# A gated delta rule at the head of a two-block network: inverses by blocks of 16 instead of 32, with the projections rearranged around them

## Chip, cores, metric

One core of a Trainium2 chip runs the whole program. The metric is the device time of one execution in microseconds, taken as the median of several runs.

## The reference, cut to what matters

The network maps 256 tokens of width 1024 through two blocks. The first layer is a gated delta net with 8 heads of width 128: four projections (q, k, v, z) of 1024 columns each, a causal depthwise convolution of 4 taps with Silu on q, k and v, the delta rule, and an output norm gated by Silu(z). All of it is fp32.

```python
proj = hn @ w_in
qkv = silu(causal_depthwise_conv(proj[..., :3072], conv_w))
z = proj[..., 3072:4096]
...
gc = cumsum(g, axis=-1)
decay = exp(where(tri_incl, gc[..., :, None] - gc[..., None, :], -inf))
a_low = where(tri_strict, einsum('bhncd,bhnsd->bhncs', k_beta, k) * decay, 0.0)
a_mat = a_low + eye(c)
sol = triangular_solve(a_mat, concat([v * beta, k_beta * exp(gc)]), lower=True, unit_diagonal=True)
...
o = rmsnorm(o, out_norm_g) * silu(z)
return o.reshape(b, t, DN_DIM) @ w_out
```

Behind it come an MLP, a block attention, a second MLP, and a second block of four mixers (among them a gated 31-tap convolution whose gate is a sigmoid, a forgetting attention and a differential attention), a cross attention and a gated MLP.

## The kernel before

Every linear layer goes through `lin` (L241) and `group`. A weight tile of 128 x 1024 (two k-slices of 512 columns) is loaded by the SP queue into `wr`, and `weight` splits it into a high part `wh` (a copy on ACT, L77) and a low part `wl` (a subtraction on DVE, L57); three matmuls per block (L53) then make up one fp32 product. The ring of weights has 4 `wr` and 5 `wh`/`wl` buffers. A group of 512 columns is four such tiles, 96 matmuls, and accumulates in two `acc` banks of PSUM. In the delta net there are just two `acc` banks, so a group can't start before the group ahead of it has been taken out of both. The other six banks (`ps`) serve everything else. The order of each engine's queue is made by a scheduler from the program order (its priorities), `later(n)` (a lower priority by n) and `after(...)` (an instruction of the same engine that has to be issued before). Each engine then works its queue in order.

The stages of `delta_net` (L447) are, in program order: `gates`; `decays` for the four pairs of (group of four heads, chunk of 128 tokens), which makes the matrix M of decays; the two k groups of projections; `unit_keys` and `gram`, which make A, 16 matrices of 128 x 128 (8 heads, 2 chunks); `inverses`; `level_64` and `level_128`; the q and v groups; `intra` (M times the products of k and q); `tokens`; `outputs`; the two z groups under `later(300)` and `later(600)`; and the output projection.

`inverses` (L567) takes the 32 x 32 blocks on the diagonal of A through HBM (`ga`, DMAs of the POOL queue) into `at`, each block on two partitions (one for its even columns, one for its odd ones), and inverts all 64 of them at once on DVE. It makes 31 steps of two dependent instructions each (`tmp`, `zt`). The result goes back through HBM (`gz`) into Z. `level_64` and `level_128` then fill the blocks below: each call transposes Z (`turned`, L600: four transposes on PE, a copy `X` on ACT), multiplies A by Z, copies `Y` on ACT, multiplies by X, and writes the negated product into Z on ACT. There are eight such calls.

`conv_pair` (L505) is what takes a q, k or v bank out: a copy into `pad` (2 buffers, their three leading columns set to zero on POOL each time), a scaled copy of the bank into `cy`, six multiply-adds on DVE (L60), and a Silu on ACT. `on_z` (L718) takes a z bank out by a clamp on DVE, Exp, Ln and Exp on ACT, and a multiply on DVE that reads the bank once more. ACT has one table of functions at a time. `table` (L271) loads the one that holds both Ln and Exp; Silu and the Sigmoid of the second block's gate (`gate` in `long_conv`, L1150) need others.

Of the kernel before, what the change touches and what calls it, by code (L numbers as in the profile page):

```python
# [16 lines left out]
P = 128  # L17
T = 256
D = 1024
KD = D // P  # L20
# [4 lines left out]
class Net:  # L25
# [421 lines left out]
    def delta_net(self):  # L447
        nc, tc, a = self.nc, self.tc, self.a
        W = a["dn_w_in"][0]
        H, d = 8, 128  # L450
        banks = self.ctx.enter_context(ExitStack())
        banks.enter_context(self.banks(2))
        with ExitStack() as ctx:
            dp = ctx.enter_context(tc.tile_pool(name="dn", bufs=1, reuse_waits="tile"))
# [46 lines left out]
            Z = core.tile([P, 16, P], F32, name="Z")  # L501
            nc.gpsimd.memset(Z, 0.0)
            four = lambda t, g, c: t[:, (g * 2 + c) * 4:(g * 2 + c) * 4 + 4, :]

            def conv_pair(col, o, dst, behind):  # L505
                t = col // P
                pad = dp.tile([P, 2, T + 3], F32, tag="pad", name="pad", bufs=2)
                nc.gpsimd.memset(pad[:, :, 0:3], 0.0)
                self.copy(pad[:, :, 3:], o)
                y = dp.tile([P, 2, T], F32, tag="cy", name="cy", bufs=2)  # L510
                w = lambda j, i: cw[:, j * 24 + t + i:j * 24 + t + i + 1]
                for i in range(2):
                    self.act(y[:, i, :], o[:, i, :], AF.Copy, scale=w(3, i))
                for j in range(3):
                    for i in range(2):
                        self.stt(y[:, i, :], pad[:, i, j:j + T], w(j, i), y[:, i, :], OP.mult, OP.add)
                with self.after(*behind):
                    self.last_silu = self.act(dst, y, AF.Silu)

            def project(dst, tag, base, g, behind):  # L520
                dst[g] = dp.tile([P, 4, T], F32, tag=tag, name=tag, bufs=2)
                base += g * 512
                self.lin(W, KD, [(base, 512)], rd, lambda col, o: conv_pair(
                    col, o, dst[g][:, (col - base) // P:(col - base) // P + 2, :], behind))

# [8 lines left out]
            def decays(g, c):  # L534

                h4 = slice(g * 4, g * 4 + 4)
# [30 lines left out]
            def inverses(sv):  # L567


                ga = hbm.tile([4, 16, 32, 32], F32, name="ga")  # L570
                gz = hbm.tile([4, 16, 32, 32], F32, name="gz")
                for b in range(4):
                    r = slice(32 * b, 32 * b + 32)
                    nc.gpsimd.dma_start(ga[b].rearrange("m i j -> i m j"), A[r, :, r])
                at = sv.tile([P, 32, 32], F32, name="at")
                for s in range(2):
                    nc.gpsimd.dma_start(at[s * 64:s * 64 + 64], ga.rearrange("b m i j -> (b m) i j"))
                zt = sv.tile([P, 16, 32], F32, name="zt")
                zi = sv.tile([P, 16, 32], I32, name="zi")
                nc.gpsimd.iota(zi, pattern=[[-2, 16], [1, 32]], base=0, channel_multiplier=0)  # L580
                zf = sv.tile([P, 16, 32], F32, name="zf")
                nc.gpsimd.tensor_copy(zf, zi)
                for s in range(2):
                    r = slice(s * 64, s * 64 + 64)
                    self.ts(zt[r], zf[r], float(s), None, OP.is_equal, eng=nc.gpsimd)
                tmp = sv.tile([P, 160], F32, name="tmp")
                for j in range(31):
                    n, m = j // 2 + 1, 31 - j
                    u = tmp[:, 0:n * m].rearrange("p (c i) -> p c i", i=m)
                    self.tt(u, zt[:, 0:n, j:j + 1].to_broadcast([P, n, m]),  # L590
                            at[:, j + 1:32, j][:, None, :].to_broadcast([P, n, m]), OP.mult)
                    self.tt(zt[:, 0:n, j + 1:32], zt[:, 0:n, j + 1:32], u, OP.subtract)
                to = gz.rearrange("b m (c s) i -> s (b m) c i", s=2)
                for s in range(2):
                    nc.gpsimd.dma_start(to[s], zt[s * 64:s * 64 + 64])
                for b in range(4):
                    r = slice(32 * b, 32 * b + 32)
                    nc.gpsimd.dma_start(Z[r, :, r], gz[b].rearrange("m c i -> c m i"))

            def turned(zz):  # L600
                X = big("X", 2)
                p = self.ps()
                for i in range(4):
                    nc.tensor.transpose(p[:, i * P:(i + 1) * P], zz[:, i, :], self.ident)  # L604
                self.copy(X, v4(p))
                return X

            def level_64(A, zz):
# [31 lines left out]
            def intra(g, c):  # L640

                cs = slice(c * P, (c + 1) * P)
                m = M[g, c]
                self.tt(m, m, b4(self.tri[:, 0:P]), OP.mult)
                p = self.ps()
                mm4(p, lambda i: (k[g][:, i, cs], q[g][:, i, cs]))
                self.tt(m, v4(p), m, OP.mult)
                if c == 1:
                    self.tt(qd[g], q[g][:, :, cs], qd[g], OP.mult)

            def tokens(g):

                h4 = slice(g * 4, g * 4 + 4)
                for c in range(2):
# [17 lines left out]
            def outputs(g):  # L672
# [22 lines left out]
                for j in range(2):  # L695
# [12 lines left out]
                    zj = z[:, g * 4 + 2 * j:g * 4 + 2 * j + 2, :]  # L708
                    self.tt(zj, o, zj, OP.mult)
# [3 lines left out]
                    self.rsqrt_wide(r, self.pairs(p), d, oeps)  # L713
                    self.tt(zj, zj, r, OP.mult)
# [3 lines left out]
            def on_z(col, o):  # L718
                h = col // P - 24
                zj = z[:, h:h + 2, :]  # L720
                e = dp.tile([P, 2, T], F32, tag="ze", name="ze", bufs=1)
# [22 lines left out]
            late = ctx.enter_context(tc.tile_pool(name="late", bufs=1, reuse_waits="tile"))  # L744
            for level in (level_64, level_128):
                for g, c in both:
                    level(four(A, g, c), four(Z, g, c))
            project(q, "q", 0, 0, behind)
            project(q, "q", 0, 1, behind)
            project(vt, "vt", 2048, 0, behind)  # L750
            project(vt, "vt", 2048, 1, behind)
            pin = self.table(self.last_silu)
            for g, c in both:
                intra(g, c)
            tokens(0)
            step = lambda it: next(it, None)
            out = [outputs(g) for g in range(2)]
            step(out[0])
            with self.later(300):
                self.lin(W, KD, [(3072, 512)], rd, on_z)  # L760
            step(out[0])
            step(out[0])
            xo[0] = (late.tile([P, 4, T], F32R, name="xoh"), late.tile([P, 4, T], F32R, name="xol"))
            with self.later(600):
                self.lin(W, KD, [(3584, 512)], rd, on_z)
            xo[1] = self.new_xg(0)
# [297 lines left out]
    def mixers(self, xg, rows, bp):  # L1064
# [539 lines left out]
```

## Time and profile before

| what | value |
|---|---|
| median of 3 runs | 1304.67 us (1304.06 to 1305.09) |
| the profiled execution | 1303.15 us |
| its span, first to last instruction | 1301.4 us |
| PE busy | 1256.0 us (97%) |
| DVE busy | 866.7 us (67%) |
| ACT busy | 739.0 us (57%) |
| POOL busy | 21.1 us (2%) |
| mean granted TensorE clock | 0.979 |
| moved by DMA | 207.31 MB, mean 159 GB/s |

Busy times overlap, so they don't add up to the span. A matmul's end is modelled, so a busy PE isn't yet a PE at its peak: the granted clock says how fast it ran (1.00 is 2.4 GHz, 0.50 is 1.2 GHz). The delta net fills the first 233 us of the span.

### The profile page before, as it was taken

The page shows a single profiled execution, that of the slowest core. Times are in us where ns is not written, and L with a number is a line of the kernel's source. Part 1 is how long each engine was busy: PE and PEld are TensorE (multiplying, and loading weights), DVE is VectorE, ACT ScalarE, POOL GpSimd, SP SyncE. Part 2 cuts the span into 40 slices and gives each one's busy share as a digit, 9 for nine tenths or more (in the row PEclk, how much of TensorE's full clock was granted, in tenths as well). Part 3 has the DMA queues.
Part 4 walks back from the last instruction along what each step waited for, and adds up shares of the span by engine and source line. Part 5 has one row for each costly group of instructions (what it writes and reads, how often), then busy time and mean ns, then how long its engine had stood idle before and what let it go on. Part 6 is the DMA issues. An engine that isn't in the chain of part 4 may idle for free.

```text
span 1301.4 us, 23746 instructions
## 1 busy us (share of the span) xinstructions
PE 1256.0 (97%) x9656; PEld 1196.5 (92%) x9656; DVE 866.7 (67%) x1388; ACT 739.0 (57%) x1132; POOL 21.1 (2%) x68
## 2 busy tenths in 40 slices
PE   7997789999999999999999999999999999999998
PEld 6997678999999999999999988799999998999997
DVE  6799236644546665744445998998556684977775
ACT  5874536654545445854545755665447565756554
POOL 2010100000000000000000000000000000000000
PEclk8998679999999999999999999999999999999999
DMA  6454303666664744656562553446664642665652
GB/s 202 143 171 146 82 1 115 227 189 189 184 181 143 224 140 142 208 171 185 179 190 69 166 176 99 145 134 192 183 190 147 203 169 65 204 201 173 184 177 83
DMA packets 99632, 207.31 MB, mean 159 GB/s; under 512 B 9694, under 2 KB 12292, under 8 KB 99524
## 3 DMA queue, kind: packets, MB, share of 16 engines
q1 hardware_dynamic: 98114, 202.85, 50.6%
q0 software_dynamic: 928, 2.88, 0.9%
q8 instruction: 75, 1.23, 0.4%
q14 instruction: 33, 0.27, 0.1%
q10 hardware_dynamic: 482, 0.08, 0.0%
HBM read 204.21 MB, written 1.57 MB: 158 GB/s over the span
## 4 chain that ended last, share of the span: by engine, by line
PE 83%; DVE 9%; ACT 3%; DMA 3%; issue 2%; POOL 0%; DVEq 0%; SPq 0%; ACTq 0%; POOLq 0%
PE acc L53 51%; PE ps L53 30%; DVE wl L57 2%; DVE yc L60 1%; ACT wh L77 1%; DMA wr<-in_mlp_w_up_dram 1%; PE ps L604 1%; DVE xl L60 1%; PE ps L894 1%; DVE sq L57 0%; DMA wr<-in_dn_w_in_dram 0%; DMA wr<-in_w_xkv_dram 0%; DMA xt<-in_x_dram 0%; DMA gz<-zt 0%; DVE tmp L57 0%
## 5 line engine op out<-in xcount | busy, mean ns | idle before, releaser
L57 DVE TENSOR_TENSOR wl<-wr,wh 128x1024 fp32r<-128x1024 f32 (+1 forms) x384 | 466.3, 1219 | 297.4 <-ACT wh L77 296.7
L77 ACT ACTIVATE wh<-wr 128x1024 fp32r<-128x1024 f32 (+1 forms) x384 | 402.3, 1053 | 387.4 <-PE acc L53 235.9
L53 PE MATMUL acc<-xh,wh 128*128 128x256 f32 (+1 forms) x1064 | 305.8, 288 | 7.8 <-DVE z L60 5.1
L53 PE MATMUL acc<-xh,wl 128*128 128x256 f32 (+1 forms) x1064 | 304.1, 287 | 3.5 <-DVE wl L57 3.5
L53 PE MATMUL acc<-xl,wh 128*128 128x256 f32 (+1 forms) x1064 | 303.8, 286 | 0.8 <-DVE xl L57 0.8
L53 PE MATMUL ps<-xh,wh 128*128 128x256 f32 (+1 forms) x872 | 248.1, 285 | 4.7 <-DVE x L57 2.5
L53 PE MATMUL ps<-xh,wl 128*128 128x256 f32 (+1 forms) x872 | 247.4, 284 | 1.8 <-DVE wl L57 1.8
L53 PE MATMUL ps<-xl,wh 128*128 128x256 f32 (+1 forms) x872 | 247.4, 284 | 0.5 <-DVE xl L57 0.3
L53 PEld LDWEIGHTS acc<-xh,wh 128*128 128x128 f32 (+1 forms) x1064 | 204.4, 192 | 11.5 <-issue 6.5
L53 PEld LDWEIGHTS acc<-xh,wl 128*128 128x128 f32 (+1 forms) x1064 | 204.3, 192 | 5.1 <-DVE wl L57 3.7
L53 PEld LDWEIGHTS acc<-xl,wh 128*128 128x128 f32 (+1 forms) x1064 | 204.7, 192 | 2.1 <-DVE xl L57 1.2
L53 PEld LDWEIGHTS ps<-xh,wh 128*128 128x128 f32 (+1 forms) x872 | 166.4, 191 | 6.0 <-DVE x L57 2.7
L53 PEld LDWEIGHTS ps<-xh,wl 128*128 128x128 f32 (+1 forms) x872 | 166.4, 191 | 2.4 <-DVE wl L57 2.0
L53 PEld LDWEIGHTS ps<-xl,wh 128*128 128x128 f32 (+1 forms) x872 | 166.5, 191 | 1.5 <-DVE xl L57 1.1
L53 PE MATMUL acc<-hh,wh 128*128 128x256 f32 x512 | 144.6, 283 | 0.0
L53 PE MATMUL acc<-hh,wl 128*128 128x256 f32 x512 | 144.3, 282 | 0.0
L53 PE MATMUL acc<-hl,wh 128*128 128x256 f32 x512 | 144.2, 282 | 0.0
L53 PEld LDWEIGHTS acc<-hh,wl 128*128 128x128 f32 x512 | 97.3, 190 | 0.0
L53 PEld LDWEIGHTS acc<-hh,wh 128*128 128x128 f32 x512 | 97.2, 190 | 0.0
L53 PEld LDWEIGHTS acc<-hl,wh 128*128 128x128 f32 x512 | 97.1, 190 | 0.0
L60 DVE SCALAR_TENSOR_TENSOR yc<-cpad,vec_b,yc 128x256 f32<-128x256 f32 x120 | 51.3, 480 | 0.1
L60 DVE SCALAR_TENSOR_TENSOR fy<-pad,vec_b,fy 128x256 f32<-128x256 f32 x88 | 36.7, 479 | 0.0
(430 smaller groups left out, 1744.7 us busy)
## 6 DMA issues: line engine op xcount, KB each, us to landing
wr<-in_mlp_w_up_dram SPq DMA_DIRECT2D x64, 512.0 KB
wr<-in_mlp_w_down_dram SPq DMA_DIRECT2D x64, 512.0 KB
wr<-in_w_in_dram SPq DMA_DIRECT2D x44, 512.0 KB
wr<-in_w_up_dram SPq DMA_DIRECT2D x44, 512.0 KB
wr<-in_dn_w_in_dram SPq DMA_DIRECT2D x32, 512.0 KB
wr<-in_w_gate_dram SPq DMA_DIRECT2D x32, 512.0 KB
wr<-in_mb_w_in_dram SPq DMA_DIRECT2D x24, 512.0 KB
wr<-in_w_down_dram SPq DMA_DIRECT2D x22, 512.0 KB
```

What stands on the lines that cost most here:

```text
L53: self.last_mm = self.nc.tensor.matmul(out, lhsT=lhsT, rhs=rhs, start=start, stop=stop, skip_group_check=True)
L57: return (eng or self.nc.vector).tensor_tensor(out=out, in0=a, in1=b, op=op)
L60: return self.nc.vector.scalar_tensor_tensor(out, a, s, b, op0=op0, op1=op1, **kw)
L77: a = self.nc.scalar.activation(hi, src, AF.Copy)
L604: nc.tensor.transpose(p[:, i * P:(i + 1) * P], zz[:, i, :], self.ident)
L894: self.nc.tensor.transpose(pt[:, i * P:(i + 1) * P], p[:, i * P:(i + 1) * P], self.ident)
```

## The change

The blocks that DVE inverts become 16 x 16: 15 steps instead of 31, 128 blocks, one per partition, and `at` shrinks to 16 columns. A third level, `level_32`, joins the blocks of 16 on PE. It takes its factors from a new tile L, which four more DMAs of the POOL queue fill from A, and `gz` is first set to zero by a DMA. The convolution works in place in its destination, out of six `pad` tiles that are zeroed once; its multiply-adds for the second q group and both v groups are held on DVE until the last step of the inverse (`hold`). z becomes one Silu out of the bank, and its norm weight moves into `outputs`. `intra` moves: group 0 ahead of the levels, group 1 behind `level_32`; its mask multiply goes to POOL, behind the last DMA of the inverse. `decays` and `tokens` put work of DVE on ACT, four instructions of 128 x 128 for one of 128 x 512. The first z group is `later(200)`, the second waits on PE for the first transpose of `level_32`. One table load follows z's Silus, and one follows the second block's sigmoids.

```diff
+            L = core.tile([P, 16, 32], F32, name="L")
+            pads = [dp.tile([P, 2, T + 3], F32, name=f"pad{i}") for i in range(6)]
...
-            def conv_pair(col, o, dst, behind):
+            def conv_pair(col, o, dst, behind, hold):
                 t = col // P
-                pad = dp.tile([P, 2, T + 3], F32, tag="pad", name="pad", bufs=2)
-                nc.gpsimd.memset(pad[:, :, 0:3], 0.0)
+                pad = pads[t // 2 % len(pads)]
                 self.copy(pad[:, :, 3:], o)
-                y = dp.tile([P, 2, T], F32, tag="cy", name="cy", bufs=2)
+                y = dst
...
-                    self.act(y[:, i, :], o[:, i, :], AF.Copy, scale=w(3, i))
+                    self.act(y[:, i, :], pad[:, i, 3:], AF.Copy, scale=w(3, i))
+                with self.after(*hold):
...
                         self.stt(y[:, i, :], pad[:, i, j:j + T], w(j, i), y[:, i, :], OP.mult, OP.add)
...
-                self.tt(m, v4(p), tok(gc[:, c, h4]), OP.subtract)
+                for i in range(4):
+                    self.act(m[:, i, :], p[:, i * P:(i + 1) * P], AF.Abs, scale=-1.0, bias=gc[:, c, g * 4 + i:g * 4 + i + 1])
...
-                self.act(m, m, AF.Abs)
...
+                nc.gpsimd.dma_start(gz.rearrange("b m i j -> (b m) (i j)"), Z[0:64].rearrange("p m i -> p (m i)")[:, 0:1024])
...
+                for b in range(4):
+                    r = slice(32 * b + 16, 32 * b + 32)
+                    nc.gpsimd.dma_start(L[r, :, 0:16], A[r, :, 32 * b:32 * b + 16])
...
-                for j in range(31):
-                    n, m = j // 2 + 1, 31 - j
+                for j in range(15):
+                    n, m = j + 1, 15 - j
...
+            def level_32(L, zz):
+                X = turned(zz)
+                p = self.ps()
+                rows = [slice(r, r + 32) for r in range(0, P, 32)]
+                for i in range(4):
+                    for r in rows:
+                        self.mm(p[r, i * 32:(i + 1) * 32], L[r, i, :], zz[r, i, r], True, True)
+                v = lambda p: p[:, 0:128].rearrange("p (h e) -> p h e", e=32)
+                Y = big("Y", 2)
+                self.copy(Y[:, :, 0:32], v(p))
+                p = self.ps()
+                for i in range(4):
+                    for r in rows:
+                        self.mm(p[r, i * 32:(i + 1) * 32], X[r, i, r], Y[r, i, 0:32], True, True)
+                for r in range(0, P, 32):
+                    self.act(zz[r:r + 16, :, r + 16:r + 32], v(p)[r:r + 16, :, 16:32], AF.Copy, scale=-1.0)
...
-                self.tt(m, m, b4(self.tri[:, 0:P]), OP.mult)
...
+                with self.after(self.back):
+                    self.tt(m, m, b4(self.tri[:, 0:P]), OP.mult, nc.gpsimd)
...
-                    self.tt(kx[c], v4(p), tok((beg if c else kdec)[:, h4]), OP.mult)
+                    for i in range(4):
+                        h = g * 4 + i
+                        self.act(kx[c][:, i, :], p[:, i * P:(i + 1) * P], AF.Copy, scale=(beg if c else kdec)[:, h:h + 1])
...
-                self.ts(e, o, -80.0, None, OP.max)
-                with tc.issue_after(pin.ins):
-                    self.act(e, e, AF.Exp, scale=-1.0)
-                self.act(e, e, AF.Ln, bias=1.0)
-                self.act(e, e, AF.Exp, scale=-1.0)
-                self.stt(zj, o, self.vec["onorm"], e, OP.mult, OP.mult)
+                with self.after(*behind):
+                    silus.append(self.act(z[:, h:h + 2, :], o, AF.Silu))
...
+            project(q, "q", 0, 0, behind)
+            hold = self.solved,
+            project(q, "q", 0, 1, behind, hold)
+            project(vt, "vt", 2048, 0, behind, hold)
+            project(vt, "vt", 2048, 1, behind, hold)
+            for c in range(2):
+                intra(0, c)
+            turns, silus = [], []
+            for level, src in ((level_32, L), (level_64, A), (level_128, A)):
                 for g, c in both:
-                    level(four(A, g, c), four(Z, g, c))
+                    level(four(src, g, c), four(Z, g, c))
+                    turns.append(self.last_turn)
+                if src is L:
+                    for c in range(2):
+                        intra(1, c)
+            with self.later(200):
+                self.lin(W, KD, [(3072, 512)], rd, on_z)
+            with self.after(turns[0]):
+                self.lin(W, KD, [(3584, 512)], rd, on_z)
+            with self.after(*silus):
+                pin = self.table(silus[-1])
             tokens(0)
...
-                    self.act(sg[:, m + i, :], sg[:, m + i, :], AF.Sigmoid, bias=V["b_glu"][:, 4 + m + i:5 + m + i])
+                    last = self.act(sg[:, m + i, :], sg[:, m + i, :], AF.Sigmoid, bias=V["b_glu"][:, 4 + m + i:5 + m + i])
+                if m == 2:
+                    self.table(last)
```

## Rows read from the trace of the kernel before

**Rows 1.** The page, busy time of the engine that fills the span

```profile
PE 1256.0 (97%) x9656; PEld 1196.5 (92%) x9656; DVE 866.7 (67%) x1388; ACT 739.0 (57%) x1132; POOL 21.1 (2%) x68
```

**Rows 2.** Busy time by stretch: stretch, length, busy (instructions) per engine, clock, DMA

```profile
91.05:102.83 11.78, 11.77 (x96) 11.56 (x96) 11.78 (x35) 7.80 (x12) 0.21 (x2) 1.00 0.16 49
102.83:143.82 40.99, 26.92 (x192) 26.20 (x193) 33.18 (x72) 20.02 (x27) 4.26 (x6) 0.89 0.61 176
143.82:172.20 28.38, 24.50 (x225) 19.39 (x225) 0.75 (x1) 12.54 (x33) 0.00 (x0) 0.50 0.02 7
172.20:178.20 6.00, 6.00 (x39) 6.00 (x39) 2.50 (x4) 0.38 (x1) 0.00 (x0) 0.70 0.00 0
178.20:229.20 51.00, 46.38 (x358) 42.39 (x357) 30.48 (x46) 28.23 (x43) 1.23 (x3) 1.00 0.27 83
```

**Rows 3.** The chain that ended last, 91 to 103 us: start, us, what

```profile
91.05 11.78 PE acc L53 x96
```

**Rows 4.** The same chain, 131 to 147 us

```profile
131.22 0.79 POOL gz L595
132.01 4.99 DMA gz<-zt
...
137.59 1.96 POOL Z L598 x3
139.55 4.14 DMA Z<-gz
143.82 1.10 PE ps L604 x4
...
145.83 0.87 PE ps L53 x16
```

**Rows 5.** DVE by groups of instructions, 87.3 to 131 us: count, busy, mean ns

```profile
L57 DVE TENSOR_TENSOR wl<-wr,wh 128x1024 fp32r<-128x1024 f32 x11 | 13.7, 1246 | 0.3 <-ACT wh L77 0.2
L60 DVE SCALAR_TENSOR_TENSOR cy<-pad,vec_a,cy 128x256 f32<-128x256 f32 x24 | 12.2, 510 | 0.3 <-ACT cy L70 0.3
L57 DVE TENSOR_TENSOR tmp<-zt,at 128x126 f32<-128x126 f32 (+22 forms) x31 | 10.5, 339 | 0.3
L57 DVE TENSOR_TENSOR zt<-zt,tmp 128x126 f32<-128x126 f32 (+22 forms) x31 | 8.4, 270 | 0.3
```

**Rows 6.** DVE in order of time: start, us, instruction

```profile
78.89 4.84 DVE L60 SCALAR_TENSOR_TENSOR cy<-pad,vec_a,cy 128x256 f32<-128x256 f32 x12 [0.36 <-ACT cy L70]
...
87.38 0.21 DVE L57 TENSOR_TENSOR tmp<-zt,at 128x31 f32<-128x31 f32 x1
...
129.03 0.26 DVE L57 TENSOR_TENSOR tmp<-zt,at 128x56 f32<-128x56 f32 x1
...
129.57 0.21 DVE L57 TENSOR_TENSOR tmp<-zt,at 128x45 f32<-128x45 f32 x1
```

**Rows 7.** DVE and POOL in order of time, 203 to 206 us

```profile
203.94 1.22 DVE L57 TENSOR_TENSOR wl<-wr,wh 128x1024 fp32r<-128x1024 f32 x1
...
204.83 0.69 POOL L145 CAST df<-di 128x384 f32<-128x384 int32 x1
```

**Rows 8.** ACT by groups of instructions, 0 to 300 us

```profile
L70 ACT ACTIVATE m<-m 128x512 f32<-128x512 f32 x8 | 4.7, 623 | 0.9 <-DVE m L57 0.9
L73 ACT ACTIVATE vec_b<-ps 128x128 f32<-128x128 f32 (+1 forms) x4 | 0.9, 261 | 0.0
```

**Rows 9.** POOL by groups of instructions, 0 to 215 us

```profile
L65 POOL TENSOR_SCALAR zt<-zf 64x512 f32<-64x512 f32 x2 | 3.0, 1496 | 0.2
...
L582 POOL CAST zf<-zi 128x512 f32<-128x512 int32 x1 | 0.6, 607 | 0.1
```

**Rows 10.** ACT in order of time, in the second block's differential attention

```profile
840.79 1.28 ACT L70 ACT_TABLE_LOAD   x1
...
842.79 1.28 ACT L70 ACT_TABLE_LOAD   x1
```

**Rows 11.** PE in order of time, the same stretch

```profile
846.45 0.30 PE L894 MATMUL ps<-ident,s 128*128 128x128 f32 x1 [2.65 <-DVE s L60]
```

More of the change, by code (lines that the diff above doesn't have):

```diff
@@ L502, in delta_net, with project @@
             nc.gpsimd.memset(Z, 0.0)
+            L = core.tile([P, 16, 32], F32, name="L")
+            nc.gpsimd.memset(L, 0.0)
+            pads = [dp.tile([P, 2, T + 3], F32, name=f"pad{i}") for i in range(6)]
+            for pad in pads:
+                nc.gpsimd.memset(pad[:, :, 0:3], 0.0)
             four = lambda t, g, c: t[:, (g * 2 + c) * 4:(g * 2 + c) * 4 + 4, :]
-            def conv_pair(col, o, dst, behind):
+            def conv_pair(col, o, dst, behind, hold):
                 t = col // P
-                pad = dp.tile([P, 2, T + 3], F32, tag="pad", name="pad", bufs=2)
-                nc.gpsimd.memset(pad[:, :, 0:3], 0.0)
+                pad = pads[t // 2 % len(pads)]
                 self.copy(pad[:, :, 3:], o)
-                y = dp.tile([P, 2, T], F32, tag="cy", name="cy", bufs=2)
+                y = dst
                 w = lambda j, i: cw[:, j * 24 + t + i:j * 24 + t + i + 1]
                 for i in range(2):
-                    self.act(y[:, i, :], o[:, i, :], AF.Copy, scale=w(3, i))
-                for j in range(3):
-                    for i in range(2):
+                    self.act(y[:, i, :], pad[:, i, 3:], AF.Copy, scale=w(3, i))
+                with self.after(*hold):
+                    for j, i in [(j, i) for j in range(3) for i in range(2)]:
                         self.stt(y[:, i, :], pad[:, i, j:j + T], w(j, i), y[:, i, :], OP.mult, OP.add)
                 with self.after(*behind):
-                    self.last_silu = self.act(dst, y, AF.Silu)
-            def project(dst, tag, base, g, behind):
+                    self.last_silu = self.act(y, y, AF.Silu)
+            def project(dst, tag, base, g, behind, hold=()):
                 dst[g] = dp.tile([P, 4, T], F32, tag=tag, name=tag, bufs=2)
@@ L523, in project @@
                 self.lin(W, KD, [(base, 512)], rd, lambda col, o: conv_pair(
-                    col, o, dst[g][:, (col - base) // P:(col - base) // P + 2, :], behind))
+                    col, o, dst[g][:, (col - base) // P:(col - base) // P + 2, :], behind, hold))
             def big(tag, bufs, pool=None):
@@ L582, in inverses @@
-                nc.gpsimd.tensor_copy(zf, zi)
[L583 to L586, printed above, removed]
-                for j in range(31):
-                    n, m = j // 2 + 1, 31 - j
+                at = sv.tile([P, 16, 32], F32, name="at")
+                flat = ga.rearrange("b m i j -> (b m) (i j)")
+                for h in range(2):
+                    r = slice(h * 64, h * 64 + 64)
+                    nc.gpsimd.dma_start(at[r].rearrange("p i j -> p (i j)")[:, 0:496], flat[:, h * 528:h * 528 + 496])
@@ L594, in inverses @@
-                for s in range(2):
-                    nc.gpsimd.dma_start(to[s], zt[s * 64:s * 64 + 64])
+                            at[:, j + 1:16, j][:, None, :].to_broadcast([P, n, m]), OP.mult)
+                    self.solved = self.tt(zt[:, 0:n, j + 1:16], zt[:, 0:n, j + 1:16], u, OP.subtract)
+                for h in range(2):
+                    q = slice(16 * h, 16 * h + 16)
+                    nc.gpsimd.dma_start(gz[:, :, q, q].rearrange("b m c i -> (b m) c i"), zt[h * 64:h * 64 + 64])
@@ L596, in inverses @@
                 for b in range(4):
                     r = slice(32 * b, 32 * b + 32)
-                    nc.gpsimd.dma_start(Z[r, :, r], gz[b].rearrange("m c i -> c m i"))
+                    self.back = nc.gpsimd.dma_start(Z[r, :, r], gz[b].rearrange("m c i -> c m i"))
             def turned(zz):
@@ L712, in outputs @@
                     r = dp.tile([P, 2, T], F32, tag="kr", name="kr", bufs=1)
-                    self.rsqrt_wide(r, self.pairs(p), d, oeps)
+                    with tc.issue_after(pin.ins):
+                        self.rsqrt_wide(r, self.pairs(p), d, oeps)
                     self.tt(zj, zj, r, OP.mult)
@@ L757, in delta_net @@
             out = [outputs(g) for g in range(2)]
[L758 to L762, printed above, removed]
+            for _ in range(3):
+                step(out[0])
             xo[0] = (late.tile([P, 4, T], F32R, name="xoh"), late.tile([P, 4, T], F32R, name="xol"))
-            with self.later(600):
-                self.lin(W, KD, [(3584, 512)], rd, on_z)
             xo[1] = self.new_xg(0)
```

31 lines of the change are left out of this document (8 added, 23 removed).

## The prediction, made before the changed kernel ran

> **What bounds it now.** I read the page first: PE is busy for 97% of the span [rows 1], so time can be won only where PE stands still or runs at its lower clock. The stretches of the delta net, read by their clock, show where that is [rows 2]. From 91.05 to 102.83 us PE is full at the full clock: the last v group is 96 matmuls in 11.78 us [rows 3]. Between 102.83 and 143.82 it is busy for only 26.92 of 40.99 us, at a clock of 0.89. From 143.82 to 172.20, in the eight calls of the two levels, the clock is 0.50 throughout, and to 178.20, in `intra`, 0.70. After that it is full again. Third, the chain of waits says what PE waited for: the last step of the inverse, then `gz` out (issue at 131.22, landed by 137.0), `Z` back (landed by 143.7), and only then the first transpose [rows 4]. So the inverse sets when the levels start. Fourth, DVE from 87.3 to 131 us: the inverse itself is 10.5 + 8.4 = 18.9 us of work [rows 5], drawn out to some 43 us, because 24 multiply-adds of the convolution (12.2 us) and 11 splits (13.7 us) stand between its steps. By 143.8 us the z groups, PE's only other work (the 192 matmuls of that stretch, [rows 2]), are used up, so the levels run alone, and at half clock.
>
> The sum is made on the profiled execution, 1303.15 us for a span of 1301.4. It lies 1.52 us under the median of 1304.67, and I add that at the end. About 0.2%, 2.6 us, is what a measurement of this kernel can tell from no change.
>
> **The inverse and its way back.** Thirty-one steps become 15, with at most 8 x 8 = 64 elements. A step of 56 elements takes 129.57 - 129.03 = 0.54 us from start to start [rows 6]. I use it for all 15: 8.1 us. The held multiply-adds can't come between, the splits can: three of 1.22 us [rows 7], as the ring fills, make 11.8 us. Group 0's products for `intra` may add 1 us. The start stays at 87.4 us [rows 6]. Two things move it, and I let them cancel: `at` no longer queues on POOL behind a zeroing of `pad` that waits for DVE, and `decays` puts four instructions of 128 x 128 on ACT (some 4 x 0.26 us) in place of one Abs of 0.62 us [rows 8], four times, 1.7 us more on the way to A. So the inverse ends at 99 us, and the issue of `gz` follows there rather than at 131.22. The way back costs what it does now, 143.82 - 131.22 = 12.6 us [rows 4]: as many pieces, half as long. The bound is 11 to 14 us. Z is there at 112 us. The four DMAs for L and the zeroing of `gz` lie beside the 15 steps on POOL's queue. I cost them at nothing. Without that cover they would cost four issues of about 0.65 us each, as the three in [rows 4].
>
> **The stall that the hold makes.** `pads[t // 2 % 6]` gives q's second group pads 2 and 3 (t // 2 = 2, 3) and v's first group pads 2 and 3 again (t // 2 = 8, 9). So v's first group can't be copied out of its banks until the held multiply-adds of q have run, and with two `acc` banks the last v group can't start. That group started at 91.05 us [rows 3]. Now it waits for 99 us, plus half of the 4.84 us that twelve multiply-adds take [rows 6], plus a copy of some 0.6 us [rows 8]: 102.0 us for the first bank, 104.4 for the second. As the first bank gives PE 12 matmuls, 1.5 us, the group ends at 104.4 + 11.78 - 1.5 = 114.7 us. What is behind v's copy on ACT's queue waits too, weight splits above all, but PE has no use for them then. Only group 0 of `intra` fits into the hole.
>
> **What PE has to do from there.** Two z groups: 2 x 11.78 = 23.6 us [rows 3]. The old levels: 24.50 us busy at a clock of 0.50 [rows 2], so 12.2 at 1.00. `level_32`, four calls: the transposes take 1.10 us at half clock, and 32 small matmuls of two passes make 64 instructions, where 16 took 0.87 us at half clock [rows 4]; at full clock that is 0.55 + 64 / 16 x 0.87 / 2 = 2.29 us, so 9.2 us. The levels together: 21.4 us. `intra` for group 1: half of 6.00 x 0.70 = 4.2, so 2.1. Sum: 114.7 + 23.6 + 21.4 + 2.1 = 161.8 us. I add 2 us for the lower clock behind the hole and for waits inside the levels: 163.8 against 178.20 now, **14.4 us** less. This holds only if z fills the levels. The calls have 163.8 - 112 = 52 us, twelve at 4.3 us each, where one took 28.38 / 8 = 3.5 us at half clock, so their chain fits. On ACT a z bank now takes one Silu, and DVE no longer reads the bank.
>
> **The rest.** `outputs` and the output projection keep their 51.00 us [rows 2]. `tokens` puts 16 instructions of about 0.26 us (4.2 us) on ACT, busy there for 28.23 us of the 51, and takes four from DVE: nothing, with bounds of -2 and +2 us. The mask on POOL has from 112 us until `outputs` to finish, so it is hidden. Its price is in no row of this kind. The one-input cast of the same shape takes 0.61 us and a tensor-scalar on half the partitions 1.50 [rows 9]. I take 1.5 us each, 6 us in all, nearer to the second since it has arithmetic in it; ends 0.6 and 3.0, the latter twice the tensor-scalar.
>
> The load behind the sigmoids should take the place of those that come in pairs later, Ln apart from Exp. One such pair shows in front of PE: loads at 840.79 and 842.79 us, 1.28 us each [rows 10], then PE idle for 2.65 us until `s` came [rows 11]. I take 2.57 us, both loads, as won; bounds 0 and 2.65.
>
> Sum: -14.4 - 2.6 = -17.0 us. The profiled execution would take 1286.1 us, the median 1287.6.
>
> **Rivals.**
>
> *No hole.* If the last v group starts at 91.05 as now, it ends at 102.83, and PE's work gives 102.83 + 23.6 + 21.4 + 4.2 + 2 = 154.0 us, so -24.2 - 2.6: **1277.9**. For it: PE had no such wait before. Against: the numbering of the pads. 20%.
>
> *DVE and POOL get in each other's way.* From 99 us on DVE has 36 held multiply-adds (14.5 us at 4.84 / 12) and about nine splits (11 us), nearly full until 125 us, and the four masks on POOL fall into just that. If each stops DVE for its length, z's splits come 6 us late (12 us at 3.0) and PE waits that long: **1293.7** (1299.7). In the trace a POOL cast of 384 elements began at 204.83 us while a DVE split ran until 205.16, and took 0.69 us [rows 7], more than the 0.61 us of 512 elements [rows 9]. One waits for the other, then, but here it was POOL. 10%. The Trainium skill, SBUF — State Buffer, section "Who interferes with whom", says that a DVE instruction with both inputs in SBUF and a GpSimd instruction that reads SBUF exclude each other, and that the one that starts first blocks the other. The trace agrees so far as those two instructions show it. The Trainium skill, GPSIMD Engine Reference, section 3.1, has 4.5 us for a two-input operation of 2048 elements, so an estimate of 1.1 us for 512; the sum would be the same by it.
>
> *Slower: the levels keep the half clock.* In `intra` and the levels PE was busy for 24.50 of 28.38 us and still had 1.2 GHz [rows 2]. If z doesn't fill them (its tiles used up before, or its two groups standing in each other's way at the two banks and the ring), PE's 21.4 + 2.1 us of work there become 47.0, with z's 23.6 in series: 185.3 us, so +7.1 - 2.6: **1309.2**. Three levels then cost more than two. It decides from about 17 of the 23.5 us at half clock on. For it: the hole of some ten microseconds lowers the clock just ahead. Against: at 112 us, v's rest and all of z are still to come, twice the work that stood beside the inverse's tail before. 10%, 8 of them slower, 2 within 0.2%.
>
> *The preload takes no later load away.* Then only -14.4: **1290.3**. 5%.
>
> **How the numbers follow.** Forecast 55%, rivals 20, 10, 10 and 5. The range reaches from just under "no hole" (1275) to 1301, the second rival's upper bound with a little beyond; outside lie the slower case and some 10% of tails. Faster by over 0.2%: 55 + 20 + 5 and 7 of the second rival's 10, as its tail may eat the gain: 87%. Same: 3 + 2 = 5. Slower: 8.
>
> **What would show it.** Right: 30 instructions of `tmp` and `zt` in about 12 us from 87 on; PE idle some ten microseconds from 91 with v's copy on ACT released by DVE's multiply-adds; the first transpose near 112; a clock near 1.00 and z's matmuls between the levels; `tokens` starting near 164; no gap of PE at the differential attention's second pair. Wrong: the inverse ending after 110; a clock of 0.50 in the levels; the z groups after the last level; PE waiting on splits beside POOL's masks.

## The result, and the profile of the changed kernel

The changed kernel takes 1282.68 us in the median of 4 runs (1282.57 to 1283.74), the kernel before 1304.88 beside it: a ratio of 0.9829 (95% interval 0.9814 to 0.9844), 22.2 us less. The forecast was 1287.6, inside a range of 1275 to 1301. The profiled execution took 1282.62 us, with a span of 1280.8; the forecast for it was 1286.1. Against the profiled execution of before that is 20.5 us less, where 17.0 were expected.

Marks along the span show where the time was won:

| mark (us from the span's start) | before | after | difference |
|---|---|---|---|
| last step of the inverse ends | 130.9 | 99.4 | -31.5 |
| last v group starts on PE | 91.05 | 102.99 | +11.9 |
| first transpose of the levels | 143.82 | 116.53 | -27.3 |
| last level matmul | 172.2 | 151.3 | -20.9 |
| output projection ends | 229.2 | 213.1 | -16.1 |
| first "down" matmul of the first MLP | 256.51 | 238.92 | -17.6 |
| table load for the second block's sigmoids | 726.14 | 708.55 | -17.6 |
| end of the span | 1301.4 | 1280.8 | -20.6 |

So 17.6 us come from the delta net and its border with the MLP, nothing from there to the sigmoids, and 3.0 us behind them. PE is still what fills the span (the page of the changed kernel):

```profile
PE 1246.9 (97%) x9928; PEld 1189.4 (93%) x9928; DVE 847.2 (66%) x1336; ACT 739.9 (58%) x1170; POOL 29.6 (2%) x71
```

It issues 272 matmuls more than before [rows 1] and is busy for 9.1 us less: the saving is in the clock and in the waits, not in the count. The stretches of the delta net, with the columns of [rows 2] (busy time per engine, granted clock, DMA):

```profile
90.50:102.99 12.49, 1.95 (x18) 1.75 (x17) 11.84 (x38) 2.19 (x4) 1.66 (x2) 0.77 0.49 134
102.99:116.69 13.70, 13.70 (x98) 13.70 (x99) 11.33 (x20) 9.05 (x15) 8.95 (x6) 0.84 0.28 82
116.53:128.36 11.83, 10.95 (x313) 9.20 (x311) 7.13 (x14) 9.89 (x28) 0.00 (x0) 1.00 0.47 159
128.29:151.26 22.97, 22.97 (x295) 19.47 (x286) 3.83 (x4) 14.26 (x37) 2.50 (x2) 1.00 0.14 47
151.26:161.00 9.74, 9.71 (x85) 9.33 (x85) 2.77 (x4) 7.22 (x21) 0.00 (x0) 1.00 0.01 2
161.00:175.13 14.13, 14.13 (x113) 13.29 (x112) 4.23 (x5) 5.57 (x8) 1.04 (x3) 1.00 0.06 12
175.00:213.10 38.10, 35.78 (x282) 33.20 (x281) 29.45 (x41) 30.20 (x44) 0.00 (x0) 1.00 0.60 193
```

The first line is new: a hole in which PE does 1.95 us of work, behind which the last v group runs at 0.84 (at 0.50 until 107.4 us, at 1.00 from there on). The third and fourth are `level_32`, `intra` of group 1 and the two old levels, all at 1.00, where before the levels stood at 0.50. DVE in order of time shows the inverse and what follows it:

```profile
87.72 1.22 DVE L57 TENSOR_TENSOR wl<-wr,wh 128x1024 fp32r<-128x1024 f32 x1 [2.58 <-ACT wh L77]
88.86 0.18 DVE L57 TENSOR_TENSOR tmp<-zt,at 128x15 f32<-128x15 f32 x1
...
94.19 0.68 DVE L57 TENSOR_TENSOR m<-ps,m 128x512 f32<-128x512 f32 x1
...
99.24 0.18 DVE L57 TENSOR_TENSOR zt<-zt,tmp 128x15 f32<-128x15 f32 x1
99.33 4.83 DVE L60 SCALAR_TENSOR_TENSOR q<-pad,vec_a,q 128x256 f32<-128x256 f32 x12
104.08 4.83 DVE L60 SCALAR_TENSOR_TENSOR vt<-pad,vec_a,vt 128x256 f32<-128x256 f32 x12
```

The inverse takes 10.6 us, with two splits and two products of `intra` inside, and the held multiply-adds of q and v begin at once behind it. The chain that ended last goes from there to the v group (start, us, what):

```profile
99.42 2.38 DVE q L60 x6
101.82 0.63 ACT q L70
102.45 0.49 ACT pad L73
102.99 13.70 PE acc L53 x96
116.69 0.44 PE ps L611 x4
```

This is the prediction's stall, with one piece more: six of q's multiply-adds, then q's Silu, which the forecast left out, the copy out of v's bank into the shared pad, and the last v group. The first transpose comes right behind v. PE doesn't wait for Z any more: Z had landed by 108.3 us.

### The profile page after: what moved, and what is told of

Its sections match the earlier page's. It is cut to its first block, busy times and chain, and to the rows that moved or that the text cites. A ratio compares the mean times of both kernels' runs of the same rounds, so it can differ in the third digit from the quotient of the medians.

```text
span 1280.8 us, 24246 instructions
## 1 busy us (share of the span) xinstructions
PE 1246.9 (97%) x9928; PEld 1189.4 (93%) x9928; DVE 847.2 (66%) x1336; ACT 739.9 (58%) x1170; POOL 29.6 (2%) x71
## 3 DMA queue, kind: packets, MB, share of 16 engines
q8 instruction: 78, 1.28, 0.4%
## 4 chain that ended last, share of the span: by engine, by line
PE 84%; DVE 8%; ACT 4%; DMA 2%; issue 2%; DVEq 0%; SPq 0%; ACTq 0%
PE acc L53 52%; PE ps L53 31%; DVE wl L57 3%; DVE yc L60 1%; DMA wr<-in_dn_w_in_dram 1%; ACT wh L77 1%; PE ps L923 1%; ACT m L70 0%; PE ps L611 0%; DMA xt<-in_x_dram 0%; DVE mx L909 0%; DVE k L60 0%; DVE xl L60 0%; DVE sq L57 0%; DVE tmp L57 0%
```

## The experiments

Each is an edit of the changed kernel, of the kernel before, or of an experiment named. Three dots stand for lines left out.

**The pads apart.** The first theory to test was that the hole comes from pads 2 and 3, which q's second group and v's first share.

```diff
-                pad = pads[t // 2 % len(pads)]
+                pad = pads[(t // 2 - (4 if t >= 16 else 0)) % len(pads)]
```

> The changed kernel with one number altered: v's four pads are numbered 4, 5, 0, 1, so that v's first group no longer shares pads 2 and 3 with q's second group. Theory (the hole of 10.5 us in front of the last v group is made by the shared pads alone): v's first group leaves its banks at once, the last v group starts near 91 us instead of 102.99, the inverse ends 1 to 3 us later than 99.4 since weight splits go on between its steps, and the time falls by 8 to 11 us, to 1272 to 1275. Rival (the hole is DVE's: whatever the pads, the group would wait for splits or for the inverse): the start moves by less than 3 us and the time stays within 2 us of 1282.7.

Measured: 1278.54 us (1276.92 to 1279.68), ratio 0.980 (0.9785 to 0.9815), between the two expectations. Its stretches, same columns:

```profile
91.70:103.10 11.40, 11.40 (x96) 11.25 (x95) 10.78 (x32) 4.56 (x7) 1.66 (x2) 1.00 0.60 177
103.10:111.60 8.50, 6.68 (x54) 6.11 (x53) 8.50 (x23) 7.95 (x14) 2.57 (x4) 1.00 0.21 44
111.60:145.30 33.70, 31.65 (x575) 26.20 (x575) 16.00 (x19) 21.81 (x60) 5.52 (x4) 1.00 0.30 96
...
190.00:200.00 10.00, 7.61 (x49) 7.20 (x48) 6.96 (x13) 4.17 (x9) 0.00 (x0) 0.83 0.66 210
```

The hole is gone, so the shared pads made it. But of its 10.5 us only 4.1 arrive. The first transpose now waits 1.1 us for Z and starts at 111.53, 5.0 us earlier: the way back of the inverse is next in line. At the end of the levels it is 6.0 us ahead (145.3), at the end of the output projection 3.0 (210.1). z's second group runs ahead of `tokens`. Behind it, from 156.5 to 210.1, PE stands still for 5.0 us, where the changed kernel lost 2.3 from the end of the levels to the end of the output projection; between 190 and 200 it is busy for only 7.61 of 10.00, at a clock of 0.83. So it looks as if the waits of `outputs` lacked z as their filler, but no run shows it.

**No hold.**

```diff
-            hold = self.solved,
+            hold = ()
```

> The changed kernel without the hold: the multiply-adds of q's second group and of v may come between the steps of the inverse again. Theory (the hold buys an early inverse at the price of the hole): no hole, but 24 to 36 multiply-adds of 0.40 us stretch the inverse to an end near 110 to 114 us, Z is back near 124, the z groups are used up by about the same time, and part of the levels runs alone at a clock of 0.50: 1285 to 1293. Rival (the hold only makes the hole, the inverse is short enough without it): 1271 to 1276.

Measured: 1282.75 us (1280.95 to 1284.27), the same as the changed kernel; both expectations missed. The 21 multiply-adds and 8 splits that now come between its steps draw the inverse out to 108.2 us; the hole goes, and a wait for Z comes in its place (the waits of PE: total, times, longest):

```profile
PE ps L611 <- DMA Z<-gz: 4.9, 1, 4.9
```

The hold moves the wait from one place to the other and is worth nothing by itself.

**No load behind the sigmoids.**

```diff
-                if m == 2:
-                    self.table(last)
```

> The changed kernel without the table load behind the second block's sigmoids. Theory: the pairs of loads for Ln and Exp come back, and with them PE's gap of 2.65 us at the differential attention: 1285 to 1286.5, with the delta net as in the changed kernel. Rival (what the second block gained came from something else): within 1 us of 1282.7.

Measured: 1285.98 us (1285.02 to 1288.43), 3.3 more. From the sigmoids to the end its span is 2.4 us longer. There are 20 table loads in it, as before the change, and 14 with the preload. PE's waits for the differential attention's `s`, first without the load:

```profile
PE ps L923 <- DVE s L60: 3.6, 3, 2.6
```

and in the changed kernel:

```profile
PE ps L923 <- DVE s L60: 1.0, 2, 0.7
```

Six loads of 1.28 us go, 7.7 us of ACT. As predicted, about what one pair costs reaches the end.

**z behind the levels.** This is the "slower" rival as a kernel.

```diff
-            with self.later(200):
+            with self.after(self.last_mm):
                 self.lin(W, KD, [(3072, 512)], rd, on_z)
-            with self.after(turns[0]):
-                self.lin(W, KD, [(3584, 512)], rd, on_z)
+                self.lin(W, KD, [(3584, 512)], rd, on_z)
```

> The changed kernel with both z groups kept on PE behind the last matmul of the levels. Theory (the levels keep the full clock only because z's matmuls fill them): the twelve calls run at a clock of 0.50 and take 43 us or more from 116.5, z comes after them with 23.6 us, and the time is 1303 to 1309, as in the slower rival of the prediction. Rival (three levels are paced by ACT's copies and not by PE's clock, and z's place matters little): the levels end before 150 us and the time is 1286 to 1291.

Measured: 1305.58 us (1303.59 to 1308.47), ratio 1.0005 (0.9995 to 1.0015): 22.9 us, the whole gain, is lost.

```profile
117.00:130.00 13.00, 8.93 (x274) 7.11 (x273) 5.44 (x12) 9.78 (x30) 0.00 (x0) 0.63 0.26 84
130.00:145.00 15.00, 12.71 (x154) 10.73 (x152) 1.38 (x2) 6.35 (x20) 2.53 (x2) 0.61 0.00 1
145.00:160.00 15.00, 12.89 (x87) 10.39 (x86) 0.00 (x0) 5.54 (x13) 0.00 (x0) 0.50 0.01 1
159.60:185.40 25.80, 25.80 (x196) 25.59 (x195) 8.58 (x7) 9.60 (x12) 0.00 (x0) 0.90 0.37 123
```

Without z between them the levels take 43 us at a clock of 0.63 to 0.50, and z stands behind them in series with 25.8 us.

**Blocks of 32 again**, with the rest of the change kept (31 steps, no `level_32`, `intra` of group 1 behind `level_64`).

```diff
-                for j in range(15):
-                    n, m = j + 1, 15 - j
+                for j in range(31):
+                    n, m = j // 2 + 1, 31 - j
...
-            for level, src in ((level_32, L), (level_64, A), (level_128, A)):
+            for level, src in ((level_64, A), (level_128, A)):
```

> The changed kernel with only the block size undone: 31 steps on blocks of 32, no level_32 (intra for group 1 behind level_64 instead), everything else as changed, the hold included. Theory (the shorter inverse pays through the hole and the way back, less the 9.2 us of PE work of the third level): the steps run from about 88 to 111 or 113 us, the last v group starts near 115 instead of 103, the two levels and z still share PE at the full clock, and the time is 3 to 7 us above the changed kernel: 1285.5 to 1290. Rival (the block size is the whole gain): 1296 or more.

Measured: 1292.92 us (1292.23 to 1294.52), ratio 0.9911, between the two. Its hole is twice as long, as its hold lasts until the 31st step (PE in order of time):

```profile
115.79 0.58 PE L53 MATMUL acc<-xh,wh 128*128 128x256 f32 x1 [22.91 <-ACT pad L73]
```

The blocks of 16 are worth 10.2 us here. The other 12 are there without them, some 3 of these by the load behind the sigmoids. The two levels of this run are those of the kernel before. With z's matmuls between them, and a v group that leads into them without a stop, they run at the full clock:

```profile
135.00:140.00 5.00, 5.00 (x77) 4.26 (x78) 1.55 (x3) 3.56 (x11) 0.00 (x0) 1.00 0.57 188
```

**The old kernel with z between its levels.** If z's matmuls are what holds the clock up, the kernel before should win most of this by a few lines:

```diff
+            turns = []
...
+                    turns.append(self.last_turn)
...
-            with self.later(600):
+            with self.later(600), self.after(turns[0]):
                 self.lin(W, KD, [(3584, 512)], rd, on_z)
```

> The kernel before, with only its second z group kept on PE behind the first transpose of level_64. Theory (what counts is matmuls left over to fill the levels): PE stands idle some 11 us longer ahead of 143.8, but the two levels, intra and z's 96 matmuls then run at the full clock in 11.8 + 12.2 + 4.2 = 28 us, to 172 instead of 178.2: 1298 to 1301. Rival (work is only moved, the idle time of before is longer by as much): 1303 to 1307.

Measured: 1312.33 us (1309.52 to 1315.85), ratio 1.0059, slower than before. Both expectations missed:

```profile
120.00:140.30 20.30, 0.00 (x0) 0.01 (x1) 10.04 (x29) 4.97 (x8) 4.25 (x6) 0.59 0.39 115
140.30:175.00 34.70, 34.68 (x263) 28.34 (x264) 1.23 (x1) 12.86 (x33) 0.00 (x0) 0.50 0.05 16
```

In the second line PE is full (34.68 of 34.70 us) and the clock is 0.50 all the way. Filling the levels isn't enough. The first line suggests why: PE came out of a hole of 20 us. Two more runs filled that hole with matmuls whose result nobody uses. For this the levels also move behind the projections in the program, and the first z group moves ahead of them, so the two runs are to be compared with each other.

```diff
-            for level in (level_64, level_128):
-                for g, c in both:
-                    level(four(A, g, c), four(Z, g, c))
...
+            with self.later(300):
+                self.lin(W, KD, [(3072, 512)], rd, on_z)
+            p = self.ps()
+            with self.after(self.last_mm):
+                for i in range(84):
+                    warm = self.mm(p[:, 0:P], self.ones, self.ones, True, True)
             turns = []
             for level in (level_64, level_128):
                 for g, c in both:
-                    level(four(A, g, c), four(Z, g, c))
+                    with self.after(*(() if turns else (warm,))):
+                        level(four(A, g, c), four(Z, g, c))
...
```

> The kernel before with its second z group behind the first transpose, as in the run before it that came out at 1312.33 us, and with one thing more: 84 matmuls of ones on ones (128x128, their result is used by nothing) stand on PE between the end of the first z group and the first transpose, so that PE doesn't stand still for the 20.65 us that Z takes to come back. Theory (the clock at which PE enters the levels decides; filling alone does not bring it back): the levels run at a clock near 1.00 with z between them, their stretch of 34.7 us becomes some 20, and the time is 1297 to 1302 us. Rival (small matmuls of 32 and 64 columns hold the clock down in the old levels whatever came before): the stretch after 140 us stays at 0.50 and the time stays at 1309 to 1315.

Measured: 1310.68 us (1310.4 to 1311.48), the rival's number. The 84 ended 1.82 us before Z came, and one microsecond into the first call, at 142.2 us, the clock fell:

```profile
130.00:140.00 10.00, 9.41 (x85) 9.22 (x83) 1.43 (x8) 0.00 (x0) 4.25 (x6) 1.00 0.24 46
140.00:142.00 2.00, 0.77 (x11) 0.63 (x11) 0.00 (x0) 0.10 (x1) 0.00 (x0) 1.00 0.14 33
142.00:143.00 1.00, 1.00 (x12) 0.73 (x10) 0.00 (x0) 0.64 (x2) 0.00 (x0) 0.61 0.06 16
143.00:150.00 7.00, 7.00 (x77) 5.48 (x76) 0.00 (x0) 2.77 (x8) 0.00 (x0) 0.50 0.00 0
150.00:160.00 10.00, 10.00 (x89) 8.50 (x88) 0.00 (x0) 3.98 (x12) 0.00 (x0) 0.50 0.01 2
```

So either that stop decided it, or these levels hold the low clock whatever stands ahead of them. The next run changed nothing but 84 to 96.

> The run with 84 matmuls of ones (1310.68 us), now with 96 of them, still used by nothing: there the 84 ended at 139.40 us, PE then stood still for 1.82 us until Z came, and the clock fell from 1.00 to 0.50 one microsecond into the first call and stayed there for 35 us, although PE was busy throughout. Theory (that stop, in front of a stretch of small matmuls, is what brings the clock down, and the level once taken is then kept, since the same five z matmuls a call ran beside a clock of 1.00 in the changed kernel): without the stop the levels run at 1.00, and the time is 1296 to 1303 us. Rival (the old levels with the old order of work hold 1.2 GHz whatever stands ahead of them): 1309 to 1313 us, with 0.50 after the first call.

Measured: 1294.83 us (1293.46 to 1296.39), ratio 0.9926 (0.991 to 0.9943), a little under the theory's range: 15.9 us less for twelve more useless matmuls, and 9.3 less than the kernel before.

```profile
141.00:142.00 1.00, 0.97 (x13) 0.79 (x13) 0.00 (x0) 0.31 (x1) 0.00 (x0) 1.00 0.00 0
142.00:143.00 1.00, 1.00 (x17) 0.87 (x17) 0.00 (x0) 0.44 (x2) 0.00 (x0) 1.00 0.00 0
143.00:150.00 7.00, 7.00 (x123) 5.98 (x118) 0.00 (x0) 4.75 (x15) 0.00 (x0) 1.00 0.01 2
150.00:160.00 10.00, 10.00 (x110) 8.17 (x108) 1.23 (x1) 6.05 (x14) 0.00 (x0) 1.00 0.19 55
```

They end at 140.40, the first transpose waits 0.62 us instead of 1.82, and the same levels, with four to six z matmuls in most calls as there, run at 1.00 to their end: 20.8 us from the first transpose on instead of 33.7. PE enters them at 1.00 in both runs, so what it does just before them decides, beside their filling. In the changed kernel the v group, which the hole pushed up against the first transpose, runs into the levels without a stop, at 1.00 from 107.4 us on.

**The subtraction of `decays` back on DVE**, on top of the pads apart. The prediction let two effects on the inverse's start cancel, and it came 1.5 us late.

```diff
-                for i in range(4):
-                    self.act(m[:, i, :], p[:, i * P:(i + 1) * P], AF.Abs, scale=-1.0, bias=gc[:, c, g * 4 + i:g * 4 + i + 1])
+                self.tt(m, v4(p), tok(gc[:, c, g * 4:g * 4 + 4]), OP.subtract)
+                self.act(m, m, AF.Abs)
```

> The kernel with v's pads renumbered (e1), and decays as in the kernel before: one subtraction on DVE and one Abs on ACT for 128 x 512, in place of four Abs of 128 x 128 on ACT. Theory (ACT is the full engine between 37 and 60 us, and its extra 1.7 us stand on the way to A and to the inverse): A, the inverse and the first transpose come 1 to 2 us earlier than in e1, and the time is 1276 to 1277.7. Rival (it is hidden by what the weights' DMAs and the matmuls of k and q set): 1278.5 within 0.7.

Measured: 1275.43 us (1273.41 to 1277.48), ratio 0.9769 (0.9752 to 0.9786), 0.6 us under the theory's range. The interval touches that of the pads apart, so the 3.1 us between the medians are likely rather than shown. The inverse starts at 85.55 us instead of 89.70, and the first transpose at 107.15 instead of 111.53. Only 1.8 us of the earlier start are the way to A that the theory names: the DMAs for `at` are issued at 77.50 us instead of 79.31. The rest is the order of DVE's queue. With the pads apart, the first step stood behind a weight split that had waited 1.92 us for its weights; here it stands ahead of that split and waits for `at` itself:

```profile
85.55 0.18 DVE L57 TENSOR_TENSOR tmp<-zt,at 128x15 f32<-128x15 f32 x1 [1.30 <-DMA at<-ga]
```

Part of the gain is lost to the clock:

```profile
107.20:112.00 4.80, 2.94 (x109) 2.29 (x107) 4.80 (x13) 2.77 (x8) 0.00 (x0) 1.00 0.00 0
112.00:115.00 3.00, 1.73 (x49) 1.41 (x37) 3.00 (x4) 2.13 (x8) 2.59 (x2) 0.65 0.02 5
115.00:120.00 5.00, 4.45 (x106) 3.35 (x105) 4.84 (x4) 2.77 (x10) 0.35 (x1) 0.50 0.43 134
120.00:125.00 5.00, 5.00 (x65) 4.50 (x64) 1.60 (x2) 2.02 (x6) 0.77 (x1) 0.69 0.84 288
```

PE stands still inside the first two calls of `level_32` (waits of 1.86 and 1.27 us for `Y`), and the clock goes down for some ten microseconds: 3 x 0.35 + 5 x 0.50 + 5 x 0.31 = 5.1 us lost at most, since PE wasn't busy all the time. Filling those waits wasn't tried.

**`kx` back on DVE too**, on top of the last one.

```diff
-                    for i in range(4):
-                        h = g * 4 + i
-                        self.act(kx[c][:, i, :], p[:, i * P:(i + 1) * P], AF.Copy, scale=(beg if c else kdec)[:, h:h + 1])
+                    self.tt(kx[c], v4(p), tok((beg if c else kdec)[:, h4]), OP.mult)
```

> The version with the pads apart and decays' subtraction back on DVE (1275.43 us), and kx in tokens back on DVE as well (one 128x512 multiply in place of four 128x128 ACTIVATE, four times). The prediction priced this part of the change at nothing, with bounds of 2 us either way. Theory: 1274.5 to 1276.5, the same time. Rival (ACT's 4.5 us of kx stand in the chain of outputs, so that taking them away gains): 1272.5 to 1274.0. The opposite (DVE is the one short of time there): 1277 to 1278.

Measured: 1275.82 us (1275.17 to 1276.5): no difference, as priced. This version and the one before it are the fastest of the study.

**z's second group later**, on top of the pads apart, so that it fills `outputs`.

```diff
-            with self.after(turns[0]):
+            with self.later(200), self.after(turns[0]):
```

> The kernel with v's pads renumbered (e1), and the second z group at the same low priority as the first, still behind the first transpose: its last matmuls go into the waits of outputs instead of ahead of tokens. Theory (the 4 us that e1 lacks against its expectation are waits of outputs that had nothing to fill them): 1274.5 to 1276.5. Rival (the norm of outputs waits for the table load behind the last z Silu, so a later z only shifts the waits): 1278 to 1281.

Measured: 1284.35 us (1279.74 to 1286.96), above both expectations; the profiled execution, at 1280.94, is one of the quicker. The theory falls: the waits get longer, since the output norm on ACT comes behind z's last Silu and the table load that follows it.

```profile
PE acc L53 <- ACT xoh L77: 6.8, 1, 6.8
```

**The mask back on DVE.**

```diff
-                with self.after(self.back):
-                    self.tt(m, m, b4(self.tri[:, 0:P]), OP.mult, nc.gpsimd)
+                if True:
+                    self.tt(m, m, b4(self.tri[:, 0:P]), OP.mult)
```

> The changed kernel with the mask of intra back on DVE, at the place where the product of k and q is multiplied (four 128x512 multiplies, some 0.69 us each, 2.8 us in all; POOL does no mask). Theory (the mask on POOL was hidden and disturbed nothing, DVE has room): two of the four stand in the held stretch, so at most 1.4 us later: 1282.5 to 1284. Rival (POOL's masks had slowed DVE's held multiply-adds, the second rival of the prediction): 1278 to 1281.

Measured: 1283.79 us (1282.39 to 1284.62), 1.1 more, inside the theory's range, though hardly more than the measurement can tell. The inverse ends at 100.88 us instead of 99.42.

## Why the prediction was right, and where it was off

*The inverse and its way back.* Predicted 87.4 to 99, measured 88.86 to 99.42. The two effects on `at` did cancel: its DMAs were issued at 78.59 us instead of 82.13, took up to 7.0 us to land instead of 4.2, and it was there at 86.2 us instead of 86.9. What came late was the first step, which stood in DVE's queue behind the split at 87.72 us and its late weights. From there two splits, not three, and two products made it 10.6 us instead of 11.8. That the end is off by only 0.4 us is luck, two misses of opposite sign. The way back took 8.6 us, from the issue at 99.72 to Z's landing at 108.3, less than the lower bound of 11 (10.7 with the pads apart, 13.9 without the hold). This miss cost nothing, since v's last group stood ahead of the first transpose in PE's queue until 116.53 us. For the same reason the sign "the first transpose near 112" failed.

*The stall that the hold makes.* Predicted to end at 102.0, measured 102.99: 0.4 us from the end of the inverse, and 0.6 from q's Silu, which stands ahead of the copy on ACT. The v group behind it ended at 116.69, not 114.7: 1 us from the start, 1 from the clock of 0.84.

*PE's work from there.* From 116.69 to 151.26 PE did the levels, `intra` of group 1, and 84 of z's 192 matmuls, which take 84 x 0.123 = 10.3 us by [rows 3]; so the levels cost 34.6 - 10.3 - 2.0 = 22.3 us, predicted 21.4. With the other 108 matmuls of z, 13.3 us, it is 47.8 us where 49.1 were predicted with the reserve.

*Which steps failed.* "`tokens` starting near 164" was wrong: it started at 151.19, because 108 of z's matmuls came behind the levels. That made the term "`outputs` and the output projection keep their 51.00 us" too high: from 151.26 to 213.1, less z's 13.3, they took 48.5. PE stands still for 2.3 us of that stretch, where it did for 4.6 us of the 51.00 [rows 2], and z's matmuls stand in the midst of it, so z seems to have filled waits there. Another 1.5 us come at the border with the MLP (16.1 less at the end of the output projection, 17.6 at the first "down" matmul), and the traces show where, though no run took that stop away. Before, PE stood still for 2.45 us there, and 0.8 us later the clock fell to 0.50, from 233.85 to 237.26 us:

```profile
233.04 0.39 PE L53 MATMUL ps<-xh,wh 128*128 128x256 f32 x1 [2.45 <-DVE x L57]
```

In the changed kernel the longest stop there is 1.19 us, and the clock stays at 1.00 (the border before, then after):

```profile
229.20:256.51 27.31, 24.86 (x194) 24.60 (x193) 18.15 (x29) 16.82 (x26) 0.00 (x0) 0.94 0.63 216
213.10:238.92 25.82, 23.67 (x195) 23.21 (x194) 16.85 (x26) 16.55 (x25) 0.00 (x0) 1.00 0.62 215
```

With 3.0 against 2.6 us behind the sigmoids, these are the 3.5 us, within 0.1, between forecast and measurement: 1.7 to the end of the output projection, 1.5 and 0.4.

*The mask on POOL.* POOL and DVE in order of time:

```profile
99.72 1.66 POOL L602 DMA_DIRECT2D gz<-zt  x2 [19.46 <-DVE zt L57]
104.10 2.58 POOL L605 DMA_DIRECT2D Z<-gz  x4 [2.73 <-issue]
106.70 5.11 POOL L57 TENSOR_TENSOR m<-m,tri 128x512 f32<-128x512 f32 x1
111.77 1.30 POOL L57 TENSOR_TENSOR m<-m,tri 128x512 f32<-128x512 f32 x1
111.94 2.21 DVE L57 TENSOR_TENSOR wl<-wr,wh 128x1024 fp32r<-128x1024 f32 x1 [1.29 <-ACT wh L77]
130.32 2.50 POOL L57 TENSOR_TENSOR m<-m,tri 128x512 f32<-128x512 f32 x2 [17.25 <-DVE m L57]
```

The masks at 130.32, where DVE was nearly idle, took 1.28 us each, against 1.5 assumed. The first one, at 106.70, came while DVE ran its multiply-adds, a product and a split back to back; it took 5.11 us and ended 1.2 us behind the last of these (110.65). DVE's twelve multiply-adds took 4.83 us, as alone [rows 6]. The second began while DVE stood idle, and now DVE paid: the split right behind it took 2.21 us instead of 1.22. The run with the pads apart has such a split of 2.23 us, the one with blocks of 32 one of 2.04. So the second rival had the conflict right and its size wrong: the two delayed each other, DVE by 1 us instead of 6, and PE waited for no split. The Trainium skill, SBUF — State Buffer, section "Who interferes with whom", says that the one that starts first blocks the other; the trace agrees in both directions, though POOL waited through several of DVE's instructions and not only the one that was running. The Trainium skill, GPSIMD Engine Reference, section 3.1, has 4.5 us for a two-input operation of 2048 elements, so an estimate of 1.1 us for 512, near the 1.28 measured.

*The rivals.* "No hole" at 1277.9 is what the pads apart gave (1278.54), but the nearness is luck, as the sum is another: without the hole PE waits for Z, and it stands still for longer in `outputs`. "The levels keep the half clock" at 1309.2 is what z behind the levels gave (1305.58, with 43 us for the levels and `intra`, where 47.0 were reckoned). Its condition was told too narrowly: it isn't only that z has to be there, PE also has to arrive without a long stop. The forecast named the hole as the danger to the clock; in the event the whole v group stood between the hole and the levels.

## What to carry to other kernels

Ask of a stretch of small matmuls at half clock not only what could fill it but what PE does just before it. A rotating buffer that both sides of a hold use turns that hold into a stop of PE; and a stop removed there brings in only what the next one in line leaves (here 4.1 of 10.5 us, with the inverse's way back next). In a queue that is worked in order, look also at what stands ahead of the first step of a chain: here it was a split whose weights came late. Work that fills waits may be missing where it was, once it is moved ahead; the traces suggest this here, and no run shows it.

## What the runs showed of the hardware that was not expected

The busy share doesn't show what the granted clock will be. With PE full at 34.68 of 34.70 us and four to six z matmuls in most calls, the levels ran at 0.50 for 35 us behind a stop of 20.65 us, and so did the same calls behind one of 1.82 us; behind one of 0.62 us they ran at 1.00. A stop of 1.13 us in front of `level_32`, in the run with the pads apart, left it at 1.00. In the kernel before, a stop of 2.45 us at the border with the MLP was followed by 3.4 us at 0.50, though PE was full behind it. Whether the length of a stop alone decides, no run shows.

A two-input multiply of 128 x 512 on POOL takes 1.28 us alone. One that came while DVE ran instructions that read two tiles back to back took 5.11 us, and such a DVE instruction that came behind a running multiply on POOL took 2.21 us instead of 1.22.
